# Sums over heads in two rounded passes, square sums on VectorE, and a final norm by square root and reciprocal, in a two-layer hybrid decoder trunk

## The chip, the cores and the metric

The kernel runs on one core of a Trainium2 chip. A core has TensorE (PE in the profile; its weight loads are listed apart as PEld), VectorE (DVE), ScalarE (ACT), GpSimd (POOL) and SyncE (SP), which here issues all DMAs. The metric is the device time of one execution in microseconds (us), as the median of several runs.

## The reference

Two layers, each with three token mixers on the same normalised input, then a last norm over the channels. Cut to what the change touches:

```python
def rms_norm(x, w):                      # at the start of a layer, and at the end
    y = xf * lax.rsqrt(jnp.mean(xf * xf, axis=-1, keepdims=True) + EPS)
    return (y * w).astype(x.dtype)

def head_norm(y, eps): ...               # retention: 4 heads of 256 channels
# RWKV, 16 heads of 64 channels:
    kk = hd(k * k_k)
    kk = kk / jnp.maximum(jnp.linalg.norm(kk, axis=-1, keepdims=True), 1e-12)
    bonus = (jnp.sum(rh * kh * r_k, axis=-1, keepdims=True) * vh)

def reference(x, ...):                   # x: 1 x 512 x 1024, float32
    for l in range(2):
        x = hybrid_layer(x, ...)         # one input projection, RG-LRU, RWKV-7, retention, output projection
    return rms_norm(x, final_norm_w)
```

## The kernel before

Activations lie with channels on the 128 partitions and the 512 tokens in the free dimension, so a row of 1024 channels is eight tiles of 128x512. A projection is eight 128x128 weight tiles against eight activation tiles. Weights and activations are split into a rounded high half and the remainder (`whi`, `wlo`; `hh`, `hl`; in the first four projections `xh`, `xl`), both in the reduced type fp32r, and each product is three matmuls: high by high, high by low, low by high. The splitting is done on the way: ScalarE copies the raw weights to `whi`, VectorE subtracts to get `wlo`. A projection is therefore 24 matmuls of 128x512.

Sums over channels run over partitions, so TensorE does them, by a matmul against a matrix of ones (`ones`) or of two 64x64 blocks of ones (`blk`). In the kernel before these take plain fp32 operands: `kss` (square norm of k per RWKV head, 16 in all), `bps` (the bonus sum, 16), `rss` (square sum of a retention head, 8) and `ss` (the square sum of a norm: 3 per norm, and two times 3 halves at the end).

Every operation is recorded through one helper, so all rows of the profile carry one line (L368 before, L378 after); the tile's name tells what it is. A planner (the class Scheduler) gives each operation a cost in the code, plays the program through by these costs, and writes the instructions of each engine out in the order that comes of it. The engines then run their own lists in order and wait by semaphores. The table `ORDER` names the order in which the pieces are recorded: `p` prepares a pair of RWKV head tiles, `s` scores, `c` its chain over chunks, `o` its output, `l` a group of RG-LRU, `r` a retention head, `b` a branch projection, and `g` two of the 24 merge gates computed ahead and stored in DRAM; nine `g` of twelve stand in the table.

At the start, `sum_sq` squares the eight tiles of x (ScalarE) and adds them to three partial sums, in layer 0 by GpSimd; three `ss` matmuls sum these; ScalarE turns the result into `rs` by Ln and Exp. Meanwhile the first four projections run on `xh`, `xl`, whose low halves VectorE makes, and are scaled by `rs` later. At the end, the last output tile is projected in two halves of 256 tokens. Each half is added to the residual (VectorE), squared (ScalarE), summed (`ss`), turned to `rs` by Ln and Exp, which are in different function tables, and then eight tiles of the half are scaled (six on VectorE, two on GpSimd) and stored.

Of the kernel before, what the change touches and what calls it, by code (L numbers as in the profile page):

```python
# [64 lines left out]

ORDER = "p0 l1 s0 g5 l0 g7 p1 g6 c0 l2 o0 g4 s1 p2 g2 g3 c1 o1 l3 s2 r0 r1 p3 g11 c2 r2 g10 o2 s3 r3 c3 g9 o3 b0 b2 b1".split()

# [84 lines left out]
class Scheduler:  # L156


    def __init__(self, nc):
        self.nc, self.pools, self.caps = nc, {}, {}  # L160
        self.ops, self._group, self._prio = [], None, 4
        self.fifo = {}

    def add_pool(self, name, pool, cap):
        self.pools[name] = pool
# [6 lines left out]
    @contextmanager  # L172
    def prio(self, p):
        old, self._prio = self._prio, p
        yield
        self._prio = old

    @contextmanager
    def group(self):
# [19 lines left out]
    def _commit(self, items):  # L199
        op = Op()  # L200
        op.i, op.eng, op.prio = len(self.ops), items[0][0], self._prio
        assert all(x[0] == op.eng for x in items)
        op.cost = sum(x[2] for x in items)
        op.calls = [(x[1], x[3], x[4]) for x in items]
        op.funcs = [x[7] for x in items if x[7]]
        op.mode = items[0][8]
        op.succ, op.ready, op.allocs, op.tiles = [], 0.0, [], []
        deps = set()
        for x in items:
            for ap in x[6]:  # L210
                self._access(op, ap, False, deps)
            for ap in x[5]:
                self._access(op, ap, True, deps)
        deps.discard(op)
        op.ndep = len(deps)
        for d in deps:
            d.succ.append(op)
        self.ops.append(op)
# [154 lines left out]
def hybrid_kernel(ctx: ExitStack, tc: tile.TileContext, xT, wt, par, cst, outT):  # L373
# [13 lines left out]
    def once(pool, name, shape, dt=F32):  # L387
        S.caps[pool][name] = 1
        return S.tile(pool, shape, dt, name, tag=name)
# [67 lines left out]
    def f32(ap):  # L457
        return ap.bitcast(F32)


    cs = once("c", "cs", [P, NRES])
    ident = cs[:, C_ID:C_ID + P]
    ones = cs[:, C_ONE:C_ONE + P]
    blk = cs[:, C_BLK:C_BLK + P]
    blkc = cs[:, C_BLKC:C_BLKC + P]
    cos = cs[:, C_COS:C_COS + T]
    sin = cs[:, C_SIN:C_SIN + T]
# [2 lines left out]
    ders = [once("c", f"der{l}", [P, NDC]) for l in range(DEPTH)]  # L470
    bcol = once("c", "bcol", [P, 4])
    warm = once("c", "warm", [P, 1])
    gsc = [once("dram", f"gs{l}", [24, P, T]) for l in range(DEPTH)]
    ysc = {(l, b): once("dram", f"ys{l}{b}", [KT, P, T]) for l in range(DEPTH) for b in range(3)}
    xsc = once("dram", "xsc", [KT, P, T])

    def pcol(l, n, i):
        return pars[l][:, POFF[n] + i:POFF[n] + i + 1]
# [6 lines left out]
    def setup():  # L485
# [21 lines left out]
                tt(lo[:, cc], raw[:, cc], f32(hi[:, cc]), ALU.subtract)  # L507
        first = hi, lo
        dma(cs[:, :C_COS], cst[:, :C_COS], P * C_COS * 4)
        dma(cs[:, C_COS:], cst[:, C_COS:NRES], P * (NRES - C_COS) * 4)  # L510
        dma(pars[1][:], par[1], P * NPC * 4)
        memset("DVE", reset[:, 0:T:CH], 0.0)
# [196 lines left out]
    def retention(l, h, n):  # L709
# [39 lines left out]
        with S.prio(3):  # L749
# [21 lines left out]
                sqs.append(sq)  # L771
            ps = tl("d", "rss")
            tt(sqs[0][:], sqs[0][:], sqs[1][:], ALU.add)
            mm(ps[:], ones, sqs[0][:], True, True, T)
            rs = sqs[0]
            act(rs[:], ps[:], ACTF.Ln, scale=1.0 / 256, bias=bcol[:, 3:4])
            act(rs[:], rs[:], ACTF.Exp, scale=-0.5)
# [34 lines left out]
    def rwkv_prep(l, la, rkv, g):  # L812
# [9 lines left out]
        for i, j in enumerate(js):  # L822
# [12 lines left out]
            thw.append(two[0])  # L835
            tha.append(two[1])
            s = tl("tp", "ksq")
            act(s[:], k[i][:], ACTF.Square, scale=pcol(l, "k_k", j))
            ps = tl("rp", "kss")
            mm(ps[:], blk, s[:], True, True, T)  # L840
            ts(thw[i][:], thw[i][:], 1.0, None, ALU.add)
            S.rec("DVE", nc.vector.tensor_tensor_scan, 1.25,
                  dict(out=thw[i][:], data0=reset[:], data1=thw[i][:], initial=0.0, op0=ALU.mult, op1=ALU.add))
# [17 lines left out]
    def rwkv_scores(l, prep, g):  # L861
# [75 lines left out]
            TB.append(tb)  # L937
        for i, j in enumerate(js):
            ps = tl("rp", "bps")
            mm(ps[:], blk, r[i][:], True, True, T)  # L940
            b = tl("tc", "bonus")
            tt(b[:], ps[:], v[i][:], ALU.mult)
            bonus.append(b)
# [213 lines left out]
    for l in range(DEPTH):  # L1157
        with S.prio(1):
            xw = gained(l, xs)
            ps = sum_sq(xs, ptt if l == 0 else tt)  # L1160
        qs = [tl("tm", "q") for _ in range(4)]
        early = [proj(l, w, xw, bank, wts=first if l == 0 and w == W_LA else None)
                 for w, bank in zip((W_LA, W_K, W_R, W_V), "aaad")]
# [76 lines left out]
    with S.prio(0):  # L1240
# [8 lines left out]
                tt(acc[k % 2][:], acc[k % 2][:], sq[:], ALU.add)  # L1249
        gain = [pcol(0, "final_norm_w", k) for k in range(KT)]  # L1250
        k, wts, rs = KT - 1, weights(l, W_OUT + KT - 1), tl("tm", "rs")
        for hf in range(2):
            cols = slice(256 * hf, 256 * hf + 256)
            ps = proj(l, None, ms, "ad"[hf], wts=wts, cols=cols)
            tt(xs[k][:, cols], xs[k][:, cols], ps[:, cols], ALU.add)
            act(sq[:, cols], xs[k][:, cols], ACTF.Square)
            act(warm[:], sq[:, 256 * hf:256 * hf + 1], ACTF.Ln, scale=0.0, bias=bcol[:, 0:1])
            ps = tl("rp", "ss")
            for n, a in enumerate(acc):
                mm(ps[:, cols], ones, a[:, cols], n == 0, n == 2, 256)  # L1260
            act(rs[:, cols], ps[:, cols], ACTF.Ln, scale=1.0 / D, bias=bcol[:, 0:1])
            act(rs[:, cols], rs[:, cols], ACTF.Exp, scale=-0.5)
            for i in range(KT):
                if i % 4 == 1:
                    if hf == 0:
                        act(xs[i], xs[i], ACTF.Identity, scale=gain[i])
                    ptt(xs[i][:, cols], xs[i][:, cols], rs[:, cols], ALU.mult)
                else:
                    stt(xs[i][:, cols], xs[i][:, cols], gain[i], rs[:, cols], ALU.mult, ALU.mult)
                dma(outT[i][:, cols], xs[i][:, cols], TILE_B // 2)  # L1270

    with tc.manual_schedule():
# [77 lines left out]
```

## Time and profile before

| | before |
|---|---|
| time, median of 3 runs (range) | 1973.65 us (1973.26 to 1974.21) |
| time of the profiled execution | 1973.38 us |
| its span in the profile | 1971.6 us |
| PE busy / DVE / ACT / POOL, share of the span | 99% / 64% / 46% / 29% |
| VectorE, busy us and instructions | 1262.5, 1887 |
| ScalarE, busy us and instructions | 914.1, 1384 |
| loads of function tables on ScalarE | 101, 1283 ns each |

A busy share is an average over the whole span; which engine sets the pace at a place is read from the idle time there and from what ended it. Matmuls are pipelined: the profile draws one longer than its turn, so the price of a matmul is read from the distance between starts. A plain fp32 matmul is issued in two parts, so it counts as two rows of the profile. The profiled execution lasts 1.8 us longer than its span.

### The profile page before, as it was taken

Reading aid. Unit: us, or ns where it says so; the run is one execution under the profiler, and the core shown is the slowest. Engines: PE = TensorE matmul, PEld = TensorE weight load, DVE = VectorE, ACT = ScalarE, POOL = GpSimd, SP = SyncE. Lnnn points to the kernel's source line nnn. Section 1 sums busy time; section 2 is a strip of 40 time slices with the busy share of each in tenths; the row PEclk is TensorE's granted clock in tenths of the full one; section 3 lists DMA queues with packets and bytes.
Section 4 is the critical chain, followed back from the end, with each engine's and each line's share of the span. In section 5 each row is a group of like instructions: output and inputs, shape, how many; then the busy total and the mean of one; then the engine's idle time right before and its main releaser. Section 6 shows DMA issues by size and latency. Waiting matters only on the chain.

```text
span 1971.6 us, 32177 instructions
## 1 busy us (share of the span) xinstructions
PE 1947.8 (99%) x12822; PEld 1544.9 (78%) x12822; DVE 1262.5 (64%) x1887; ACT 914.1 (46%) x1384; POOL 574.4 (29%) x797
## 2 busy tenths in 40 slices
PE   8999999999999999999999999999999999999997
PEld 5788778877787888788878887788787878777886
DVE  8894676667645855365569847756685468544554
ACT  6763753554325434242357638335534452434333
POOL 3138122612541154000012452253317121720000
PEclk9999999999999999999999999999999999999999
DMA  4233233322231325264522331333132313434642
GB/s 153 91 110 126 73 108 111 115 73 82 82 119 54 105 73 160 89 228 133 176 94 94 123 118 64 111 107 113 49 100 96 103 50 111 134 98 140 219 144 75
DMA packets 110981, 217.08 MB, mean 110 GB/s; under 512 B 43376, under 2 KB 46704, under 8 KB 110832
## 3 DMA queue, kind: packets, MB, share of 16 engines
q1 hardware_dynamic: 110832, 215.03, 33.7%
q8 instruction: 101, 1.65, 0.3%
q14 instruction: 48, 0.39, 0.1%
HBM read 184.58 MB, written 30.41 MB: 109 GB/s over the span
## 4 chain that ended last, share of the span: by engine, by line
PE 95%; DVE 3%; issue 0%; ACT 0%; DMA 0%; SPq 0%; DVEq 0%; ACTq 0%
PE acc L368 71%; PE p L368 5%; PE vp L368 5%; PE gate L368 2%; PE rsc L368 2%; PE sc L368 2%; PE rout L368 2%; PE w L368 2%; PE yt L368 1%; PE vt L368 1%; PE lora L368 1%; PE tr L368 1%; PE bps L368 1%; PE kss L368 1%; DVE wlo L368 0%
## 5 line engine op out<-in xcount | busy, mean ns | idle before, releaser
L368 PE MATMUL acc<-hh,whi 128*128 128x512 f32 x1488 | 604.8, 406 | 0.0
L368 ACT ACTIVATE whi<-raw 128x1024 fp32r<-128x1024 f32 (+1 forms) x283 | 298.8, 1056 | 638.0 <-PE acc L368 519.8
L368 PE MATMUL acc<-hh,wlo 128*128 128x512 f32 x1488 | 581.3, 391 | 1.3 <-DVE wlo L368 1.3
L368 PE MATMUL acc<-hl,whi 128*128 128x512 f32 x1488 | 580.4, 390 | 0.0
L368 DVE TENSOR_TENSOR wlo<-raw,whi 128x1024 fp32r<-128x1024 f32 (+1 forms) x283 | 358.3, 1266 | 186.7 <-ACT whi L368 183.4
L368 PEld LDWEIGHTS acc<-hh,whi 128*128 128x128 f32 x1488 | 279.3, 188 | 68.5 <-issue 7.2
L368 PEld LDWEIGHTS acc<-hh,wlo 128*128 128x128 f32 x1488 | 279.3, 188 | 62.1 <-DVE wlo L368 2.2
L368 PEld LDWEIGHTS acc<-hl,whi 128*128 128x128 f32 x1488 | 279.7, 188 | 57.2 <-issue 4.3
L368 POOL TENSOR_TENSOR etmp<-ex,ea 64x31 f32<-64x31 f32 (+15 forms) x248 | 170.2, 686 | 44.6 <-DMA ea<-ead 25.8
L368 POOL TENSOR_TENSOR dec<-sv,pc 64x128 f32<-64x128 f32 x96 | 50.3, 524 | 438.5 <-DVE sv L368 434.9
L368 POOL TENSOR_TENSOR ex<-ex,etmp 64x31 f32<-64x31 f32 (+15 forms) x248 | 168.8, 681 | 19.4
L368 ACT ACT_TABLE_LOAD x101 | 129.6, 1283 | 3.4 <-DVE pc L368 0.9
L368 PE MATMUL acc<-yh,whi 128*128 128x512 f32 x256 | 104.1, 407 | 0.0
L368 PE MATMUL acc<-yh,wlo 128*128 128x512 f32 x256 | 100.2, 391 | 0.0
L368 PE MATMUL acc<-ylo,whi 128*128 128x512 f32 x256 | 99.9, 390 | 0.0
L368 POOL TENSOR_TENSOR bk<-k,pi 64x512 f32<-64x512 f32 x32 | 50.9, 1589 | 162.7 <-DVE k L368 147.9
L368 PE MATMUL acc<-mq,whi 128*128 128x512 f32 (+1 forms) x272 | 79.9, 377 | 0.0
L368 PE MATMUL acc<-yq,whi 128*128 128x512 f32 x256 | 78.8, 389 | 0.0
L368 PE MATMUL vp<-whi,hh 128*128 128x256 f32 x256 | 78.2, 305 | 0.0
L368 DVE TENSOR_SCALAR sv<-p 64x128 f32<-64x128 f32 x64 | 18.8, 295 | 90.7 <-ACT sv L368 71.9
L368 PE MATMUL vp<-whi,hl 128*128 128x256 f32 x256 | 72.3, 282 | 0.0
L368 PE MATMUL vp<-wlo,hh 128*128 128x256 f32 x256 | 72.3, 282 | 0.0
(229 smaller groups left out, 3168.9 us busy)
## 6 DMA issues: line engine op xcount, KB each, us to landing
raw<-in_w SPq DMA_DIRECT2D x281, 512.0 KB, 3.3
yl<-ys SPq DMA_DIRECT2D x48, 256.0 KB, 4.8
gs<-thm SPq DMA_DIRECT2D x36, 256.0 KB, 2.3
thm<-gs SPq DMA_DIRECT2D x36, 256.0 KB, 4.0
ys<-thg SPq DMA_DIRECT2D x16, 256.0 KB, 2.5
ys<-bonus SPq DMA_DIRECT2D x16, 256.0 KB, 2.4
ys<-yr SPq DMA_DIRECT2D x16, 256.0 KB, 2.4
x<-in_x SPq DMA_DIRECT2D x8, 256.0 KB, 4.3
```

The source lines that it names most:

```text
L368: fn(*[r(v) for v in pos], **{k: r(v) for k, v in kw.items()})
```

## The change

Four things change. (1) A function `column_sums` does the sums `kss`, `bps` and `rss` with a high half `csh` (ScalarE) and a remainder `csl` (VectorE), both fp32r, in two matmuls against `picks`, an fp32r copy of the matrices of ones made once at the start. The `ss` sums stay as they are. (2) The square sums of layer 0 are added by VectorE. (3) The final norm takes Sqrt on ScalarE and a reciprocal on VectorE; the scalings of both halves are recorded behind both sums, and `behind` holds VectorE's scalings so that all but the first two of half 0 stand behind the addition of half 1. (4) `ORDER` places other gates elsewhere: nine `g` as before, with g1 in the place of g9. The remaining diff:

```diff
-ORDER = "p0 l1 s0 g5 l0 g7 p1 g6 c0 l2 o0 g4 s1 p2 g2 g3 c1 o1 l3 s2 r0 r1 p3 g11 c2 r2 g10 o2 s3 r3 c3 g9 o3 b0 b2 b1".split()
+ORDER = "p0 l1 s0 g5 l0 g11 g7 g6 p1 c0 l2 o0 g4 s1 g3 g1 p2 c1 o1 l3 s2 r0 r1 p3 c2 r2 g10 o2 s3 g2 r3 c3 o3 b0 b2 b1".split()
...
+        if self._behind is not None and self._behind.eng == op.eng:
+            deps.add(self._behind)
...
+    def column_sums(ps, w, s, pool, hi=None):
+        if hi is None:
+            hi = tl(pool, "csh", dt=F32R)
+            act(hi[:], s, ACTF.Copy)
+        lo = tl(pool, "csl", dt=F32R)
+        tt(lo[:], s, f32(hi[:]), ALU.subtract)
+        with S.group():
+            mm(ps, w, hi[:], True, False, T)
+            mm(ps, w, lo[:], False, True, T)
...
+        act(picks[:], cs[:, C_ONE:C_ONE + 2 * P], ACTF.Copy)
...
-            mm(ps[:], ones, sqs[0][:], True, True, T)
+            column_sums(ps[:], onesr, sqs[0][:], "tm")
...
+            act(hi[:], k[i][:], ACTF.Square, scale=pcol(l, "k_k", j))
-            mm(ps[:], blk, s[:], True, True, T)
+            column_sums(ps[:], blkr, s[:], "tp", hi)
...
-            mm(ps[:], blk, r[i][:], True, True, T)
+            column_sums(ps[:], blkr, r[i][:], "tp")
...
-            ps = sum_sq(xs, ptt if l == 0 else tt)
+            ps = sum_sq(xs, tt)
...
-            act(warm[:], sq[:, 256 * hf:256 * hf + 1], ACTF.Ln, scale=0.0, bias=bcol[:, 0:1])
+            if hf == 0:
+                act(warm[:], sq[:, 0:1], ACTF.Sqrt)
...
-            act(rs[:, cols], ps[:, cols], ACTF.Ln, scale=1.0 / D, bias=bcol[:, 0:1])
-            act(rs[:, cols], rs[:, cols], ACTF.Exp, scale=-0.5)
+            act(rs[:, cols], ps[:, cols], ACTF.Sqrt, scale=1.0 / D, bias=bcol[:, 0:1])
+            S.rec("DVE", nc.vector.reciprocal, 0.45, dict(out=rs[:, cols], in_=rs[:, cols]))
+        for hf, cols in enumerate(halves):
...
-                    stt(xs[i][:, cols], xs[i][:, cols], gain[i], rs[:, cols], ALU.mult, ALU.mult)
+                    with S.behind(added[1] if hf == 0 and i > 2 else added[0]):
+                        stt(xs[i][:, cols], xs[i][:, cols], gain[i], rs[:, cols], ALU.mult, ALU.mult)
```

In the order of the instructions it looks so at three places. First, TensorE at the first `kss` of layer 0, before, between the last matmul of one projection and the first of the next:

```order
L368 MATMUL acc_609<-hh_454,whi_573 128x512
L368 MATMUL acc_609<-hl_467,whi_573 128x512
L368 MATMUL acc_609<-hh_454,wlo_587 128x512
L368 MATMUL kss_651<-ksq_641,cs_214 128x512
L368 MATMUL acc_655<-hh_340,whi_616 128x512
L368 MATMUL acc_655<-hl_357,whi_616 128x512
```

and now:

```order
L378 MATMUL acc_611<-hh_417,wlo_586 128x512
L378 MATMUL acc_657<-hh_319,whi_618 128x512
L378 MATMUL acc_657<-hl_346,whi_618 128x512
L378 MATMUL acc_657<-hh_319,wlo_628 128x512
L378 MATMUL acc_657<-hh_348,whi_618 128x512
L378 MATMUL acc_657<-hl_360,whi_618 128x512
L378 MATMUL acc_657<-hh_348,wlo_628 128x512
L378 MATMUL kss_668<-csh_646,picks_244 128x512
L378 MATMUL kss_668<-csl_655,picks_244 128x512
```

The one fp32 matmul has become two fp32r matmuls, and they stand six projection matmuls later. Second, the start of the program on VectorE, from the third low half of x on (`sq` the square sums, `sp` and `der` small constants), before:

```order
L368 SCALAR_TENSOR_TENSOR xl_173<-x_121,par0_139,xh_165 128x512
L368 TENSOR_SCALAR der0_150<-par0_139 128x8
L368 TENSOR_SCALAR der0_150<-par0_139 128x24
L368 TENSOR_TENSOR sp0_152<-par0_139,sp0_152 128x8
L368 SCALAR_TENSOR_TENSOR xl_193<-x_133,par0_139,xh_176 128x512
L368 TENSOR_SCALAR sp0_152<-sp0_152 128x8
L368 SCALAR_TENSOR_TENSOR xl_200<-x_133,par0_139,xh_195 128x512
L368 TENSOR_TENSOR wlo_157<-raw_136,whi_147 128x512
L368 SCALAR_TENSOR_TENSOR xl_216<-x_145,par0_139,xh_203 128x512
```

and now, from the same low half up to the last one but one:

```order
L378 SCALAR_TENSOR_TENSOR xl_173<-x_121,par0_139,xh_164 128x512
L378 TENSOR_TENSOR sq_141<-sq_141,sq_170 128x512
L378 SCALAR_TENSOR_TENSOR xl_190<-x_133,par0_139,xh_176 128x512
L378 TENSOR_TENSOR sq_160<-sq_160,sq_181 128x512
L378 SCALAR_TENSOR_TENSOR xl_198<-x_133,par0_139,xh_192 128x512
L378 TENSOR_TENSOR wlo_157<-raw_136,whi_147 128x512
L378 SCALAR_TENSOR_TENSOR xl_214<-x_145,par0_139,xh_200 128x512
L378 TENSOR_TENSOR sq_141<-sq_141,sq_202 128x512
L378 SCALAR_TENSOR_TENSOR xl_223<-x_145,par0_139,xh_216 128x512
L378 TENSOR_TENSOR sq_141<-sq_141,sq_221 128x512
L378 TENSOR_TENSOR sq_160<-sq_160,sq_212 128x512
L378 TENSOR_TENSOR wlo_240<-raw_179,whi_225 128x1024
```

Five additions of squares have come between the low halves, and the small constants have gone behind them; the low half of the next weights (`wlo_240`) now stands ahead of the last two low halves of x. On TensorE the three `ss` matmuls, which stood behind all 24 matmuls of the first projection, now stand behind 18 of them, and the first six matmuls of the second projection come before the last six of the first. Third, the end of the program on VectorE (`xr` the residual tiles, of which each name holds two), before:

```order
L368 TENSOR_TENSOR xr_17245<-xr_17245,acc_17472 128x256
L368 SCALAR_TENSOR_TENSOR xr_17245<-xr_17245,par0_139,rs_17519 128x256
L368 SCALAR_TENSOR_TENSOR xr_17218<-xr_17218,par0_139,rs_17519 128x256
L368 SCALAR_TENSOR_TENSOR xr_17230<-xr_17230,par0_139,rs_17519 128x256 x2
L368 SCALAR_TENSOR_TENSOR xr_17233<-xr_17233,par0_139,rs_17519 128x256
L368 TENSOR_TENSOR xr_17245<-xr_17245,acc_17512 128x256
L368 SCALAR_TENSOR_TENSOR xr_17245<-xr_17245,par0_139,rs_17519 128x256
```

and now:

```order
L378 RECIPROCAL rs_17721<-rs_17721 128x256
L378 SCALAR_TENSOR_TENSOR xr_17420<-xr_17420,par0_139,rs_17721 128x256
L378 SCALAR_TENSOR_TENSOR xr_17432<-xr_17432,par0_139,rs_17721 128x256
L378 TENSOR_TENSOR xr_17447<-xr_17447,acc_17714 128x256
L378 SCALAR_TENSOR_TENSOR xr_17432<-xr_17432,par0_139,rs_17721 128x256
L378 SCALAR_TENSOR_TENSOR xr_17435<-xr_17435,par0_139,rs_17721 128x256
L378 SCALAR_TENSOR_TENSOR xr_17447<-xr_17447,par0_139,rs_17721 128x256
L378 RECIPROCAL rs_17721<-rs_17721 128x256
```

The addition of half 1 (the second TENSOR_TENSOR before, the only one now) stood behind five scalings of half 0 and stands behind two, and each half's `rs` is finished by a reciprocal. Behind the rows shown stand six more scalings before, and seven now. On ScalarE four table loads around these norms have become one.

## Rows read from the trace of the kernel before

**Rows 1.** The page, part 1: busy us, share, instructions.
```profile
PE 1947.8 (99%) x12822; PEld 1544.9 (78%) x12822; DVE 1262.5 (64%) x1887; ACT 914.1 (46%) x1384; POOL 574.4 (29%) x797
```
**Rows 2.** The chain that ended last, by engine.
```profile
PE 95%; DVE 3%; issue 0%; ACT 0%; DMA 0%; SPq 0%; DVEq 0%; ACTq 0%
```
**Rows 3.** Busy time by stretch: start:end, length, PE, PEld, DVE, ACT, POOL, granted clock, DMA.
```profile
10.00:20.00 10.00, 6.34 (x15) 3.64 (x14) 10.00 (x12) 7.89 (x14) 7.25 (x5) 0.66 0.54 194
80.00:100.00 20.00, 20.00 (x110) 16.14 (x109) 19.80 (x29) 14.89 (x21) 3.78 (x2) 1.00 0.32 103
60.00:1000.00 940.00, 938.63 (x6264) 746.24 (x6263) 601.14 (x878) 436.98 (x663) 276.13 (x389) 1.00 0.34 111
1020.00:1940.00 920.00, 918.77 (x6181) 730.74 (x6181) 585.25 (x857) 422.02 (x641) 273.48 (x388) 1.00 0.34 109
```
**Rows 4.** TensorE around the first kss: start, us, instruction.
```profile
63.64 0.40 PE L368 MATMUL acc<-hh,wlo 128*128 128x512 f32 x1
63.87 1.02 PE L368 MATMUL kss<-ksq,cs 128*128 128x512 f32 x2
...
64.97 0.40 PE L368 MATMUL acc<-hl,whi 128*128 128x512 f32 x1
```
**Rows 5.** The chain in order of time, one piece near the end of layer 0.
```profile
858.64 126.71 PE acc L368 x558
```
**Rows 6.** The three sums by tile: count of parts, ns, first and last start.
```profile
L368 PE MATMUL kss<-ksq,cs x32: 590/592/697, 63.9 to 1580.3; 128*128 128x512 f32 x32
L368 PE MATMUL bps<-r,cs x32: 592/592/593, 137.9 to 1682.7; 128*128 128x512 f32 x32
L368 PE MATMUL rss<-ysq,cs x16: 590/592/697, 456.6 to 1701.8; 128*128 128x512 f32 x16
```
**Rows 7.** Groups by line, the split of another tile: busy, mean ns, idle before.
```profile
L368 ACT ACTIVATE cvh<-cv 128x512 fp32r<-128x512 f32 x16 | 10.1, 629 | 29.8 <-DVE cv L368 29.8
L368 DVE TENSOR_TENSOR cvl<-cv,cvh 128x512 fp32r<-128x512 f32 x16 | 12.4, 778 | 6.1 <-ACT cvh L368 6.1
```
**Rows 8.** GpSimd, VectorE and TensorE at the start, in order of time.
```profile
12.02 5.59 POOL L368 TENSOR_TENSOR sq<-sq 128x512 f32<-128x512 f32 x3 [0.35 <-ACT sq L368]
...
7.04 0.69 DVE L368 TENSOR_TENSOR wlo<-raw,whi 128x512 fp32r<-128x512 f32 x1
...
12.28 1.25 DVE L368 TENSOR_SCALAR sp<-sp 128x8 f32<-128x8 f32 x1
13.44 0.74 DVE L368 SCALAR_TENSOR_TENSOR xl<-x,par,xh 128x512 fp32r<-128x512 f32 x1
...
14.70 4.77 DVE L368 SCALAR_TENSOR_TENSOR xl<-x,par,xh 128x512 fp32r<-128x512 f32 x4
...
23.82 0.40 PE L368 MATMUL acc<-xl,whi 128*128 128x512 f32 x1
```
**Rows 9.** ScalarE, VectorE and TensorE at the end, in order of time, by engine.
```profile
1954.77 0.46 ACT L368 ACTIVATE rs<-ss,bcol 128x256 f32<-128x256 f32 x1
...
1960.36 0.42 ACT L368 ACTIVATE sq<-xr 128x256 f32<-128x256 f32 x1 [3.40 <-DVE xr L368]
...
1956.99 3.00 DVE L368 SCALAR_TENSOR_TENSOR xr<-xr,par,rs 128x256 f32<-128x256 f32 x5 [4.18 <-ACT rs L368]
1959.92 0.41 DVE L368 TENSOR_TENSOR xr<-xr,acc 128x256 f32<-128x256 f32 x1
...
1964.50 3.50 DVE L368 SCALAR_TENSOR_TENSOR xr<-xr,par,rs 128x256 f32<-128x256 f32 x6 [3.78 <-ACT rs L368]
...
1957.09 0.28 PE L368 MATMUL acc<-mq,wlo 128*128 128x256 f32 x1
1960.83 0.70 PE L368 MATMUL ss<-sq,cs 128*128 128x256 f32 x2 [3.45 <-ACT sq L368]
```
**Rows 10.** The small constants by tile: count, ns (least, median, most), first and last start.
```profile
L368 DVE TENSOR_TENSOR sp<-sp x20: 154/167/169, 21.0 to 56.1; 128x8 f32<-128x8 f32 x20
...
L368 DVE RECIPROCAL sp<-sp x2: 196/199/202, 20.7 to 47.5; 128x8 f32<-128x8 f32 x2
```

More of the change, by code (lines that the diff above doesn't have):

```diff
@@ L162, in __init__ @@
         self.fifo = {}
+        self._behind = None
     def add_pool(self, name, pool, cap):
@@ L176, in prio, with behind @@
         self._prio = old
+    @contextmanager
+    def behind(self, op):
+        self._behind = op
+        yield
+        self._behind = None
     @contextmanager
@@ L463, in hybrid_kernel @@
     ones = cs[:, C_ONE:C_ONE + P]
-    blk = cs[:, C_BLK:C_BLK + P]
     blkc = cs[:, C_BLKC:C_BLKC + P]
@@ L472, in hybrid_kernel @@
     warm = once("c", "warm", [P, 1])
+    picks = once("c", "picks", [P, 2 * P], F32R)
+    onesr, blkr = picks[:, :P], picks[:, P:]
     gsc = [once("dram", f"gs{l}", [24, P, T]) for l in range(DEPTH)]
@@ L837, in rwkv_prep @@
             s = tl("tp", "ksq")
+            hi = tl("tp", "csh", dt=F32R)
             act(s[:], k[i][:], ACTF.Square, scale=pcol(l, "k_k", j))
+            act(hi[:], k[i][:], ACTF.Square, scale=pcol(l, "k_k", j))
             ps = tl("rp", "kss")
-            mm(ps[:], blk, s[:], True, True, T)
+            column_sums(ps[:], blkr, s[:], "tp", hi)
             ts(thw[i][:], thw[i][:], 1.0, None, ALU.add)
@@ L1251, in hybrid_kernel @@
         k, wts, rs = KT - 1, weights(l, W_OUT + KT - 1), tl("tm", "rs")
-        for hf in range(2):
-            cols = slice(256 * hf, 256 * hf + 256)
+        halves = [slice(0, 256), slice(256, 512)]
+        added = []
+        for hf, cols in enumerate(halves):
             ps = proj(l, None, ms, "ad"[hf], wts=wts, cols=cols)
             tt(xs[k][:, cols], xs[k][:, cols], ps[:, cols], ALU.add)
+            added.append(S.ops[-1])
             act(sq[:, cols], xs[k][:, cols], ACTF.Square)
-            act(warm[:], sq[:, 256 * hf:256 * hf + 1], ACTF.Ln, scale=0.0, bias=bcol[:, 0:1])
+            if hf == 0:
+                act(warm[:], sq[:, 0:1], ACTF.Sqrt)
             ps = tl("rp", "ss")
@@ L1260, in hybrid_kernel @@
                 mm(ps[:, cols], ones, a[:, cols], n == 0, n == 2, 256)
-            act(rs[:, cols], ps[:, cols], ACTF.Ln, scale=1.0 / D, bias=bcol[:, 0:1])
-            act(rs[:, cols], rs[:, cols], ACTF.Exp, scale=-0.5)
+            act(rs[:, cols], ps[:, cols], ACTF.Sqrt, scale=1.0 / D, bias=bcol[:, 0:1])
+            S.rec("DVE", nc.vector.reciprocal, 0.45, dict(out=rs[:, cols], in_=rs[:, cols]))
+        for hf, cols in enumerate(halves):
             for i in range(KT):
```

## The prediction

> **What bounds the kernel now.** I read the page first: TensorE is busy 99% of the span and no other engine passes 64% [rows 1]. A busy share alone proves little, since matmul rows overlap, so I went on to the chain of work that ended last: 95% of it is TensorE's [rows 2]. The third view is busy time by stretch. From 60 to 1000 us TensorE stands idle 1.4 us (940.00 less 938.63), from 1020 to 1940 us 1.2 us, at the full granted clock [rows 3]. So between the ramps at both ends TensorE's own work is the time: a microsecond of it removed is a microsecond gained, as long as its operands keep up, and a microsecond moved onto VectorE or ScalarE costs nothing where these have room. They have it on average (64% and 46%), but not everywhere: from 80 to 100 us VectorE is busy 19.80 of 20 us [rows 3]. The two ends are other regimes: at the start VectorE makes what TensorE waits for, and at the end a chain of single operations runs with TensorE idle.
>
> **The sums over heads.** In the timeline a matmul's price is the distance of starts. From the last projection matmul before the first `kss` to the second one after it, 1.33 us pass (63.64 to 64.97) [rows 4]. Without the sum these would be two ordinary distances; 558 projection matmuls in a row take 126.71 us, 0.227 each [rows 5]. So the fp32 sum costs 1.33 - 0.454 = 0.876 us, what there is of a change between fp32 and fp32r included. Now it is two fp32r matmuls of the same 128x512 shape, at 0.227 each as those in [rows 5], 0.454 together. Saved: 0.42 us. The profile has 32, 32 and 16 parts of `kss`, `bps` and `rss`, two parts to a sum, hence 40 sums [rows 6]; they last alike (592 ns median), so one price serves. **40 x 0.42 = 16.8 us.** The starts are rounded to 0.01 us; 0.40 and 0.43 per sum as bounds give 16.0 to 17.2.
>
> What this adds elsewhere: 40 high halves on ScalarE and 40 remainders on VectorE, for which the nearest rows are the same split of another tile, 629 and 778 ns [rows 7], about 25 and 31 us. The work that hides them is TensorE's projections, which need neither engine while they run; VectorE goes from 1262 to about 1297 us of 1953. I cost them at nothing. Were the cover gone, a sum would wait for its high half, its remainder and two handoffs, 1.4 us (0.63 + 0.78). At the first `kss` the planner has put six matmuls (6 x 0.227 = 1.36 us) between the sum's old place and its new one, which is about that chain. The gates set elsewhere by `ORDER` are nine stored pairs as before, so the same matmuls and DMAs, cost nothing; the bounds are the 2.6 us of idle time in the two long stretches, which could go, and new waits (below).
>
> **The start.** Before, GpSimd adds the squares until 17.6 us (12.02 + 5.59), and while it does VectorE is slow: a constant of 8 columns takes 1.25 us at 12.28 us, where an operation of that size otherwise takes 0.17 [rows 8, 10], and four low halves of x take 4.77 us where one alone takes 0.74 [rows 8]. With the additions on VectorE that ends: the four low halves alone give back 4.8 - 4 x 0.7 = 2.0 us and each stretched constant 1.1 us, and five additions cost, priced like a low half, 5 x 0.7 = 3.5 us. That is about even, so the last low half stays near 19.5 us (14.70 + 4.77). What changes is TensorE's order: the three fp32 `ss` matmuls fill the wait for the last two low halves. From 7.04 us [rows 8] VectorE has two half splits of weights, six low halves and five additions to do ahead of the sum, 13 x 0.66 = 8.6 us, so `ss` can start at 15.8 us, if the eighth square is there, as I assume. The granted clock of 10 to 20 us is 0.66 [rows 3], part of it at 1.2 GHz: TensorE had worked in bursts with waits between. The bursts stay about as they are, so I let the clock fall again until about 20 us; then `ss` takes three times 0.876 doubled, 5.2 us, to 21.0. Of the 48 matmuls of the first two projections 30 are then left. Before, TensorE was at the second matmul of the second projection at 23.82 us [rows 8], so it had 24 left at 23.6. Thirty left at 21.0 are 24 left at 22.4 (6 x 0.227). **Gain 1.2 us.** Bounds: nothing, if the squares come late; 3.8 us, if the clock is full while `ss` runs (2.6 us less).
>
> **The end.** The last matmul of half 1 ends at 1957.4 us, but its addition waits on VectorE behind five scalings of half 0 until 1959.92; then follow square, table load, Ln, table load and Exp, and the first scaling of half 1 starts at 1964.50, the sixth ends at 1968.0 [rows 9]. Now Sqrt starts where Ln did, 1954.77, and takes the same 0.46. The reciprocal of 256 columns has no row; the nearest is one of 8 columns, 199 ns against 167 for a plain operation of that size [rows 10]. If the 32 ns are fixed, 256 columns take the 0.41 of an addition of that width [rows 9] and 0.03, 0.45 us; if they grow with the columns (4 ns each), 0.41 + 256 x 0.004 = 1.45 us; by the widest pair of those rows (202 and 154 ns, 6 ns a column) 0.41 + 1.54 = 1.95 us. I take 1.45, the middle row of the same instruction. Then: reciprocal to 1956.7; two scalings of 0.60 (3.00 for five) to 1957.9; addition to 1958.3; square (0.42) to 1958.8; `ss` (0.70) to 1959.5; Sqrt (0.46) to 1960.0, with no table load left, while VectorE does three scalings; reciprocal to 1961.5; seven scalings at 0.58 (3.50 for six) to 1965.5, against 1968.0. **Gain 2.5 us.** With 0.45 for the reciprocal the addition can start at 1957.4 and the end is 1964.1, a gain of 3.9. Stores follow the last scaling as before.
>
> The Trainium skill (VectorE: DVE Perf Modes, First, the fixed hardware budget) says that the reciprocal is an iterated divide with a repeat count of 8; at the clock given there that would be an estimated 2.2 us for 256 columns. At 8 columns it would be about 58 ns above a plain operation; the row shows 32, so the trace bears it out by half.
>
> **Sum.** 16.8 + 1.2 + 2.5 = 20.5 us off the profiled execution's 1973.38 us: 1952.9 us. The median of the runs is 0.27 us above that execution, so I forecast **1953 us** for the median.
>
> **The rivals.** (a) *The reciprocal is slow by its width*, 1.95 us a half: the addition then ends at 1958.8, the second reciprocal runs from 1960.5 to 1962.4, the last scaling ends at 1966.5, and the end gains 1.5 instead of 2.5: 1954 us. For it: it is dearer at 8 columns already; against it: only by 32 ns in the middle. The Trainium skill's repeat count, quoted above, belongs to this rival; by its estimate of 2.2 us the end would gain 1.0. (b) *The ends give more*: full clock under `ss` (2.6 more) and a fixed reciprocal (1.4 more): 1949 us. For it: TensorE now waits less between the bursts; against it: 10 to 20 us were at 0.66 and the low halves still set the pace. (c) *Some sums wait for their remainder.* VectorE works in order, and the remainder may stand behind the split of a weight tile; at 0.25 us a sum 10 us are lost: 1963 us. For it: the full stretch at 80 to 100 us; against it: 1.4 and 1.2 us of idle time in all the rest of a program planned in the same manner. (d) *Slower:* the whole new chain of 1.4 us is exposed at each sum, on TensorE's path: 40 x 1.4 = 56 us, so about 2009 us; it decides from 20.5 / 40 = 0.5 us a sum on. Against it is the room of a third of VectorE's time and the later place of the sum. (e) *The two passes are no cheaper than the one*, because a change of operand type costs what they save: only the ends remain, 1969.6 us. Against it: the changes of type alone would have to make 0.42 of the 0.876 us of [rows 4].
>
> **How the numbers follow.** Forecast 0.50, (a) 0.20, (b) 0.12, (c) 0.12, (d) 0.04, (e) 0.02. The time is that of the likeliest. The low end takes (b) with the 2.6 us of idle time gone: 1953 - 4.0 - 2.6 = 1946.4. The high end is (c), 1963, rounded down to 1962, since most of (c) lies lower. The likeliest case alone spans 1950 to 1956. A change of 0.2%, 3.9 us, is about what measurement tells from none. Slower by more than that is (d), 0.03 of it; the same is the rest of (d), a far end of (c) and part of (e), 0.03; faster is all else, 0.94.
>
> **What would show it.** Right: `kss`, `bps` and `rss` as two matmuls each 0.23 us apart, 0.42 us less around each; TensorE idle from 60 to 1940 us still under 5 us; the first scaling of half 1 some 3 us earlier than 1964.50; VectorE's 8-column operations at 0.17 us before 20 us. Wrong: waits of TensorE for `csl`, or for `wlo` where a `csl` stands ahead of it; a reciprocal that takes over 2 us; `ss` at 0.43 us a pass and the first projection ending after 24 us. The prediction falls if idle time on TensorE grows by over 10 us, wherever it lies.

## The result and the profile after

The changed kernel takes 1960.38 us (median of 4 runs, 1959.80 to 1961.27) where the kernel before takes 1973.56 in the same session: ratio 0.9935, 95% interval 0.9922 to 0.9948, 13.2 us less. The forecast was 1953, with 1946.5 to 1962 as its range: the sign and the range hold, but a third of the 20.5 us is missing.

The page, part 1, of the changed kernel:

```profile
PE 1932.9 (99%) x12822; PEld 1541.6 (79%) x12822; DVE 1296.6 (66%) x1934; ACT 907.9 (46%) x1403; POOL 552.1 (28%) x792
```

And its busy time by stretch, columns as in [rows 3]:

```profile
10.00:20.00 10.00, 9.04 (x30) 5.36 (x31) 8.65 (x25) 9.96 (x16) 0.00 (x0) 1.00 0.80 282
80.00:100.00 20.00, 19.07 (x104) 15.30 (x103) 19.75 (x28) 15.50 (x21) 7.06 (x8) 1.00 0.28 92
60.00:1000.00 940.00, 935.28 (x6277) 747.58 (x6276) 623.63 (x902) 435.67 (x674) 272.85 (x391) 1.00 0.34 111
1020.00:1926.00 906.00, 901.89 (x6135) 720.95 (x6134) 596.10 (x871) 418.02 (x648) 265.73 (x388) 1.00 0.34 109
```

TensorE has 14.9 us less work than in [rows 1]. But it now stands idle 4.7 us from 60 to 1000 and 4.1 us in the stretch of layer 1, where [rows 3] had 1.4 and 1.2. From 10 to 20 us the granted clock is 1.00, where it was 0.66. Whom TensorE waits for, in the list of waits (us in total, times, longest), in layers and ends together:

```profile
PE p L378 <- DVE zs L378: 3.4, 5, 0.9
PE sc L378 <- POOL bk L378: 1.9, 2, 0.9
PE ss L378 <- ACT sq L378: 1.8, 1, 1.8
PE acc L378 <- DVE xl L378: 1.7, 5, 0.5
PE p L378 <- DVE sv L378: 1.6, 2, 0.8
...
PE acc L378 <- DVE wlo L378: 1.1, 2, 0.6
PE gate L378 <- DVE cvl L378: 0.9, 2, 0.5
```

In the kernel before, the same list has only two rows that lie in the layers:

```profile
PE p L368 <- DVE zs L368: 2.2, 2, 1.1
PE acc L368 <- DVE wlo L368: 1.3, 2, 0.7
```

No row says that a sum waits for `csl` or `csh`, and the wait for `wlo` has not grown. The new waits are those of the chain (`p`, 5.0 us in all where it was 2.2), of the scores (`sc`), where GpSimd's `bk` is late, and of the LRU gates. The sums themselves do what was forecast; TensorE in order of time at the first `kss`, to be read beside [rows 4]:

```profile
59.63 0.40 PE L378 MATMUL acc<-hh,wlo 128*128 128x512 f32 x1
59.87 0.39 PE L378 MATMUL kss<-csh,picks 128*128 128x512 f32 x1
60.10 0.39 PE L378 MATMUL kss<-csl,picks 128*128 128x512 f32 x1
60.33 0.40 PE L378 MATMUL acc<-hh,whi 128*128 128x512 f32 x1
60.56 0.40 PE L378 MATMUL acc<-hl,whi 128*128 128x512 f32 x1
```

59.63 to 60.56 is 0.93 us where 1.33 us passed before: 0.40 less. The start, VectorE and TensorE in order of time, beside [rows 8]:

```profile
16.73 0.24 DVE L378 TENSOR_SCALAR der<-par 128x8 f32<-128x8 f32 x2
18.17 0.75 DVE L378 SCALAR_TENSOR_TENSOR xl<-x,par,xh 128x512 fp32r<-128x512 f32 x1 [0.92 <-ACT xh L378]
...
14.47 2.84 PE L378 MATMUL ss<-sq,cs 128*128 128x512 f32 x6
...
34.85 0.39 PE L378 MATMUL acc<-hh,whi 128*128 128x512 f32 x1
```

And the end, VectorE and ScalarE, beside [rows 9]:

```profile
1943.82 1.75 DVE L378 RECIPROCAL rs<-rs 128x256 f32<-128x256 f32 x1 [2.36 <-ACT rs L378]
1945.61 1.35 DVE L378 SCALAR_TENSOR_TENSOR xr<-xr,par,rs 128x256 f32<-128x256 f32 x2
1946.88 0.41 DVE L378 TENSOR_TENSOR xr<-xr,acc 128x256 f32<-128x256 f32 x1
1947.21 1.40 DVE L378 SCALAR_TENSOR_TENSOR xr<-xr,par,rs 128x256 f32<-128x256 f32 x3
1949.03 1.75 DVE L378 RECIPROCAL rs<-rs 128x256 f32<-128x256 f32 x1 [0.42 <-ACT rs L378]
1950.70 3.70 DVE L378 SCALAR_TENSOR_TENSOR xr<-xr,par,rs 128x256 f32<-128x256 f32 x7
...
1948.53 0.47 ACT L378 ACTIVATE rs<-ss,bcol 128x256 f32<-128x256 f32 x1 [0.79 <-PE ss L378]
```

To compare kernels, the span is cut into three: the *start* up to TensorE's first matmul with `hh`, the *middle* from there to the first `ss` matmul of the final norm, and the *end*. *Idle* is TensorE's idle time ahead of the middle's matmuls, added up. It is a lower bound of the waits: a projection matmul is drawn 0.39 us long while the next may start 0.23 us after it, so each wait hides up to 0.16 us. Medians and ratios are over all runs, the three parts are of the one profiled execution, which can lie off its kernel's median: 2.4 us below it for sums_own3, 1.8 to 2.3 us above it for sums_only, after_prices and best. All kernels below stand here once:

| kernel | us | ratio to before (95%) | start | middle | idle | end |
|---|---|---|---|---|---|---|
| before | 1973.56 | | 39.96 | 1912.23 | 3.9 | 19.42 |
| changed | 1960.38 | 0.9935 (0.9922 to 0.9948) | 34.85 | 1905.99 | 9.9 | 17.17 |
| sums_only | 2014.40 | 1.0204 (1.0187 to 1.0221) | 40.63 | 1953.94 | 42.6 | 19.82 |
| order_only | 1977.31 | 1.0015 (1.0006 to 1.0025) | 39.37 | 1916.22 | 7.1 | 19.42 |
| start_only | 1968.78 | 0.9975 (0.9964 to 0.9985) | 35.57 | 1911.86 | 3.7 | 19.43 |
| end_only | 1971.36 | 0.9986 (0.9977 to 0.9996) | 40.54 | 1911.91 | 3.9 | 17.23 |
| sums_own3 | 1972.36 | 0.9993 (0.9984 to 1.0003) | 39.16 | 1909.57 | 13.5 | 19.44 |
| same_order_no_csl | 1959.66 | 0.9930 (0.9915 to 0.9945) | 35.27 | 1904.94 | 9.1 | 17.18 |
| same_order_two_csl | 1967.70 | 0.9971 (0.9960 to 0.9983) | 35.35 | 1913.58 | 13.3 | 17.17 |
| same_order_fp32_sums | 1975.68 | 1.0011 (1.0002 to 1.0020) | 35.83 | 1921.02 | 9.2 | 17.17 |
| same_order_no_recip | 1957.86 | 0.9921 (0.9906 to 0.9936) | 35.76 | 1906.68 | 10.3 | 14.50 |
| after_prices | 1978.39 | 1.0028 (1.0017 to 1.0039) | 35.48 | 1926.48 | 19.9 | 16.85 |
| own3_prices_old_order | 1970.74 | 0.9986 (0.9977 to 0.9995) | 35.80 | 1915.52 | 12.9 | 16.86 |
| best | 1958.43 | 0.9925 (0.9913 to 0.9938) | 35.80 | 1908.41 | 8.6 | 14.39 |

So the change won 5.1 us at the start (forecast 1.2), 2.25 at the end (forecast 2.5), and 6.2 in the middle (forecast 16.8). The middle is what has to be explained.

### The profile page after: what moved, and what is told of

It reads as the page before. It is cut to its first block, busy times and chain, and to the rows that moved or that the text cites. A ratio compares the mean times of both kernels' runs of the same rounds, so it can differ in the third digit from the quotient of the medians.

```text
span 1958.0 us, 32282 instructions
## 1 busy us (share of the span) xinstructions
PE 1932.9 (99%) x12822; PEld 1541.6 (79%) x12822; DVE 1296.6 (66%) x1934; ACT 907.9 (46%) x1403; POOL 552.1 (28%) x792
## 5 line engine op out<-in xcount | busy, mean ns | idle before, releaser
L378 DVE TENSOR_TENSOR wlo<-raw,whi 128x1024 fp32r<-128x1024 f32 (+1 forms) x283 | 362.3, 1280 | 239.7 <-ACT whi L378 236.8
L378 POOL TENSOR_TENSOR etmp<-ex,ea 64x31 f32<-64x31 f32 (+15 forms) x248 | 161.0, 649 | 42.2 <-DMA ea<-ead 23.4
L378 ACT ACT_TABLE_LOAD x82 | 105.2, 1283 | 2.2 <-PEq L1371 0.7
L378 POOL TENSOR_TENSOR hl<-hf,hh 128x512 fp32r<-128x512 f32 x8 | 16.2, 2035 | 211.0 <-ACT hh L378 211.0
```

What stands on the lines that cost most here:

```text
L378: fn(*[r(v) for v in pos], **{k: r(v) for k, v in kw.items()})
```

## The experiments

**Each part alone.** Theory 1: VectorE's 40 remainders make it late where it is full, and TensorE waits there. Theory 2: the new `ORDER` brings the waits. Theory 3: the planner writes another order after any edit, and waits come with it. The first kernel takes all of `column_sums` and `picks` into the kernel before, the others one line or one block each:

```diff
 # sums_only
+            column_sums(ps[:], blkr, s[:], "tp", hi)
-            mm(ps[:], blk, s[:], True, True, T)
 # order_only: the new ORDER; start_only:
-            ps = sum_sq(xs, ptt if l == 0 else tt)
+            ps = sum_sq(xs, tt)
 # end_only: the block of the final norm and behind()
```

> The kernel before with column_sums and picks alone; ORDER, square sums and final norm as before. Theory 1 (the 40 remainders make VectorE late at its full stretches, so TensorE waits at other operations): about 16 us less in TensorE's own work and 8 to 10 us of new waits at sc, gate and p, so 1966 to 1968 us. Theory 2 (the new ORDER brings the waits): no new waits, 1957 to 1958 us. Theory 3 (every edit makes the planner write another order, and waits come and go with it): anything between, with waits at other places than in the changed kernel.

> The kernel before with the new ORDER alone. Theory 1: within 2 us of 1973.6 us. Theory 2: 8 to 10 us slower, 1982 to 1984 us, with waits at sc near 91 us and at gate near 123 us. Theory 3: off by some 2 to 5 us either way.

> The kernel before with the square sums of layer 0 on VectorE alone. If the start's gain is its own (full granted clock from 10 to 20 us): 5 us less, 1968.5 us, with the first product of hh near 35 us. By the prediction's step (clock falls again): 1.2 us less, 1972.4 us. Theories 1 and 2: no new waits in the middle. Theory 3: the middle moves by 2 us or more, though no instruction there was changed.

> The kernel before with the final norm by Sqrt and reciprocal and with the additions ahead of the scalings, alone. All theories of the middle: 2.2 to 2.5 us less, 1971.2 us, the reciprocal of 256 columns 1.75 us as in the changed kernel. Theory 3: the middle moves as well.

The two ends are independent: start_only gives 4.8 us (1973.64 less 1968.78, the median of before in that session), end_only 2.3, and neither touches the middle (0.4 us at most). That speaks against theory 3 in its widest form: an edit at an end leaves the middle alone. order_only costs 3.7 us, inside the range of theory 3 and of no other. And sums_only, the part from which most of the gain was to come, is 41 us *slower*, which no theory had. Alone the four parts add up to +37; together they give -13. The sums and the new `ORDER` are no independent edits. In sums_only the loss lies in a few places. Busy time by stretch there:

```profile
270.00:290.00 20.00, 19.42 (x181) 14.86 (x180) 12.02 (x18) 9.11 (x16) 8.96 (x9) 1.00 0.33 119
290.00:310.00 20.00, 7.43 (x48) 6.01 (x50) 17.13 (x29) 2.95 (x6) 3.93 (x4) 0.64 0.19 59
310.00:320.00 10.00, 10.00 (x51) 7.91 (x50) 5.67 (x12) 0.61 (x2) 0.94 (x2) 0.70 0.01 2
```

And two of TensorE's waits in that stretch, in order of time:

```profile
301.81 1.94 PE L368 MATMUL tr<-cs,bk 128*128 128x128 f32 x8 [3.99 <-DVE bk L368]
307.71 0.79 PE L368 MATMUL sc<-se,bk 64*128 64x128 f32 x2 [3.96 <-POOL bk L368]
```

For 20 us TensorE has nothing but the scores of one group and their transposes: no projection stands between, and each step waits for VectorE or GpSimd. On top the granted clock falls to 0.64 and stays at 0.70 after the stall, so part of the work behind it runs at 1.2 GHz: projection matmuls start 0.43 us apart from 312.0 to 315.8 us, and 0.23 apart from 316.1 on. Both come again in layer 1.

**Where the projections went.** A pool hands its buffers out in the order in which tiles are recorded: the planner lets an instruction take a buffer only if its tile is the first in the pool's queue (`if n >= len(free[k]) or n >= len(f) or f[n] is not t: return None`). `csh` and `csl` stand in the queues of `tp` and `tm`, which the inputs of other stages also use. Theory 4: that queue, and not the work, makes the hole.

```diff
-    caps = {"h": 16, "tp": 16, "tc": 6, "tm": 16, ...
+    caps = {"h": 16, "tp": 16, "tc": 6, "tm": 14, ..., "ch": 3}
-            hi = tl(pool, "csh", dt=F32R)
+            hi = tl("ch", "csh", dt=F32R)
-        lo = tl(pool, "csl", dt=F32R)
+        lo = tl("ch", "csl", dt=F32R)
```

> The kernel before with column_sums and picks and its own ORDER, as in sums_only, but the halves csh and csl in three buffers of their own instead of the shared pools tp and tm (tm gives up two of its 16). Theory 4 (the loss of sums_only comes from the queue for buffers: each pool hands its buffers out in the order in which tiles are recorded, and csh and csl stand in that queue ahead of what the projections need): the stretch near 283 to 310 us with nothing but score matmuls on TensorE is gone, 1965 to 1978 us. Theory 1 (VectorE's and ScalarE's added work does it): the added work is the same, so it stays within 10 us of 2014 us. Theory 2 (the old ORDER does it): 2014 us as well.

1972.36 against 2014.40: 42 us come back with the same instructions, the same old `ORDER` and only other buffers. Theory 4 stands for the loss of sums_only, and theories 1 and 2 fall there. (That the tiles' place in the queue does it is read from the planner's code; the run shows that the buffers alone decide.) The middle without idle time is now 1909.57 - 13.47 = 1896.1 us, as in the changed kernel (1905.99 - 9.95 = 1896.0), and 12.2 less than before (1908.3). But 13.5 us of idle time remain, so the sums gain little net here: 1.0 us by the median against the kernel before in the same session, 2.7 in the middle of the trace.

**One engine's work changed, every order kept.** To separate what an engine has to do from the order in which the planner puts it, three kernels keep the changed kernel's order of instructions on every engine and alter one thing as the instructions are written out:

```diff
+                if kw["out"].t.name == "csl": continue               # no_csl
+                if kw["rhs"].t.name == "csl": kw = dict(kw, rhs=op.calls[0][1]["rhs"])
...
+                for _ in range(1 + (kw["out"].t.name == "csl")):     # two_csl
...
+                if kw["rhs"].t.name == "csl": continue               # fp32_sums
+                if kw["rhs"].t.name == "csh":
+                    kw = dict(kw, lhsT=kw["lhsT"].bitcast(F32), rhs=kw["rhs"].bitcast(F32), stop=True)
```

> The changed kernel with every engine's instructions in the order in which they stand there, but the 40 subtractions csl left out, and the second matmul of each sum reading csh again (the sums then lack their remainder): TensorE's work is the same, VectorE has some 30 us less. Theory 1 (the new waits come from VectorE's added work): 7 to 9 us less, 1952 to 1954 us, no wait at sc near 91 us, TensorE idle under 3 us from 60 to 1000. Theory 3 (the waits belong to the arrangement that the planner wrote, whatever VectorE does): within 2.5 us of 1960.4 us, the waits at sc, gate and p still there.

> The changed kernel with every instruction in the order in which it stands there, but each of the 40 subtractions csl done twice: some 30 us more on VectorE. Theory 1: the waits at the full stretches grow by what is added there, at least 8 us more, 1968 us or above. Theory 3: VectorE has room, 1960 to 1963 us.

> The changed kernel with every instruction in the order in which it stands there, high halves and subtractions included, but each of the 40 sums as one fp32 matmul again, of the high half alone (the sums then lack their remainder): only TensorE's work differs, by 40 times 0.42 us, 16.8 us. If the new waits belong to the arrangement, whatever TensorE does: 16 to 17 us more than the changed kernel, 1976 to 1977.5 us, with the waits at sc, gate and p as they are. If they are the time saved at the sums, handed back where VectorE, ScalarE and GpSimd set the pace (TensorE now comes too early there): only 7 to 11 us more, 1967 to 1971 us, and the waits at sc near 91 us, at gate and at p shrink or are gone.

Without the 40 subtractions the time is 1959.66 us, 0.7 less, which is hardly to be told from nothing. TensorE's list of waits in that kernel:

```profile
PE p L382 <- DVE zs L382: 2.8, 4, 0.9
...
PE sc L382 <- POOL bk L382: 1.9, 2, 0.9
...
PE p L382 <- DVE sv L382: 1.6, 2, 0.8
...
PE gate L382 <- DVE cvl L382: 0.9, 2, 0.4
```

They are the waits of the changed kernel, less one `p` on `zs` (2.8 us where it was 3.4). Theory 1 falls. But the room is thin: with the subtractions done twice the time is 7.3 us more, since the next 30 us on VectorE do show. Theory 3's "1960 to 1963" misses that by far, and theory 1's "1968 us or above" only by 0.3: the second 30 us behave as theory 1 had it for the first. In the sums' own rows TensorE now waits for a remainder (`PE rss L379 <- DVE csl L379: 0.5, 2, 0.3` stands in its list).

With fp32 sums again in the same order the middle is 1921.02 - 1905.99 = 15.0 us longer, 0.376 us a sum, and the total 15.3 us longer (16 to 17 if the waits belong to the arrangement, 7 to 11 if they are time handed back). Its waits:

```profile
PE p L382 <- DVE zs L382: 3.3, 5, 0.9
PE sc L382 <- POOL bk L382: 1.9, 2, 1.0
...
PE p L382 <- DVE sv L382: 0.9, 2, 0.4
PE gate L382 <- DVE cvl L382: 0.9, 2, 0.5
```

TensorE comes 15 us later to the end and waits at the same places as long, except at one `p` of each layer (0.44 instead of 0.79 us). So the time saved at the sums is not handed back at the waits; they belong to the arrangement. This kernel also prices it: TensorE has the same matmuls as in the kernel before, and the middle is 1921.02 - 1912.23 = 8.8 us longer. With the -15.0 of the sums that makes the -6.2 of the middle; it is no check, since the 8.8 is the remainder. It holds all else that the change does there: the place of every instruction, the subtractions (0.7 us above) and the 40 high halves on ScalarE, which no run took out alone. Of the 8.8 us, 5.3 are idle time (9.2 against 3.9). For the other 3.5 the traces name no wait; hidden waits could make them, or changes between kinds of operand, since TensorE goes back from fp32 to fp32r 293 times there and 269 times before (counted in the traces). Which of the two it is stays open, as no run prices a change alone. Two executions of the same middle differ by up to 0.7 us (changed, same_order_no_recip).

**The reciprocal.** Again every order kept; Sqrt and reciprocal of the final norm become one activation.

```diff
+                if fn == self.nc.vector.reciprocal and kw["out"].size == 256: continue
+                if kw.get("func") == ACTF.Sqrt and kw["out"].t.name in ("rs", "warm"):
+                    kw = dict(kw, func=ACTF.Abs_reciprocal_sqrt)
```

> The changed kernel with every instruction in the order in which it stands there, but rs of the final norm made by one activation (Abs_reciprocal_sqrt) where Sqrt and a reciprocal on VectorE stood. If the reciprocal stands on the path at both halves: half 0 gives 0.8 us (the addition of half 1 then waits for TensorE), half 1 the 1.75 us of the reciprocal, 2.5 us together, 1957.9 us. If only the second counts: 1.75 us, 1958.6 us. If the activation brings table loads that the warming does not cover: nothing or up to 2.5 us more, 1960 to 1963 us.

1957.86 us, 2.5 less, as worked out for a reciprocal that stands on the path at both halves. VectorE's end in order of time:

```profile
1945.41 1.36 DVE L382 SCALAR_TENSOR_TENSOR xr<-xr,par,rs 128x256 f32<-128x256 f32 x2 [2.36 <-ACT rs L382]
1947.65 0.42 DVE L382 TENSOR_TENSOR xr<-xr,acc 128x256 f32<-128x256 f32 x1 [0.88 <-PE acc L382]
1947.99 1.67 DVE L382 SCALAR_TENSOR_TENSOR xr<-xr,par,rs 128x256 f32<-128x256 f32 x4
1949.82 3.49 DVE L382 SCALAR_TENSOR_TENSOR xr<-xr,par,rs 128x256 f32<-128x256 f32 x6 [0.17 <-ACT rs L382]
```

The addition of half 1 now waits for TensorE alone, and the second `rs` costs VectorE 0.17 us of waiting.

**Prices.** If the waits are planned in, are they planned on wrong prices? The planner believes that `bk` on GpSimd lasts 1.39 us; the trace has 1.62. The next kernels give it the durations of the changed kernel's trace; the second also has the old `ORDER` and the three buffers of sums_own3, the third these buffers, another `ORDER` and the one activation of same_order_no_recip.

```diff
+        if aps_w and eng in ("DVE", "ACT", "POOL"):
+            cost = PRICE.get(f"{eng} {aps_w[0].t.name} {getattr(aps_w[0], 'size', 0)}", cost - 0.05)
```

> The changed kernel, its ORDER and its computation as they are; only the planner's prices for VectorE, ScalarE and GpSimd are set to the mean durations that its own trace shows, less 0.05 us for the overlap of one instruction with the next (bk on GpSimd 1.57 instead of 1.39, r 1.14 instead of 0.73, bk on VectorE 0.82 instead of 0.68, and so on for 70 groups). Theory 3 in its narrower form (the new waits are operations that last longer than the planner believes, where TensorE's cover was planned to the tenth of a microsecond): the waits at sc near 91 us, gate near 123 us and p are planned away, 954 to 957 us above 1000, that is 1954 to 1957 us; a wait at a sum may come in their place. If prices have nothing to do with it: 1960 us or above, with waits of the same size at other places.

> The changed kernel with the ORDER of before, the measured prices of after_prices, and csh and csl in three buffers of their own (tm 14 instead of 16). Theory 4 with theory 3 (what the old ORDER lost in sums_only was the queue for buffers, and the rest prices): 1957 to 1964 us, 50 us below sums_only. Theory 2 (the split sums need the new ORDER as such): 1975 us or above.

> The changed kernel with everything that the runs so far point to: csh and csl in three buffers of their own, measured prices, rs of the final norm by one activation, and an ORDER chosen for these (p0 g4 l1 s0 g7 l0 g11 g6 p1 c0 g5 l2 o0 s1 g3 p2 c1 g10 g1 o1 and so on, again nine gates). If theories 3 and 4 are right: TensorE idle under 3 us from 60 to 1900 us as in the kernel before, the sums at 0.45 us each, 1947 to 1951 us. If waits come back whatever the prices: 1955 us or above.

All three miss what theories 3 and 4 had for them. after_prices is 18 us *slower* than the changed kernel: the wait at `sc` on `bk` is planned away, and others stand in its place, the longest at a sum. TensorE there in order of time:

```profile
645.18 0.51 PE L454 MATMUL rss<-csh,picks 128*128 128x512 f32 x1 [1.05 <-ACT csh L454]
648.36 0.79 PE L454 MATMUL rss<-csl,picks 128*128 128x512 f32 x1 [2.68 <-DVE csl L454]
```

And the stretch around it:

```profile
640.00:660.00 20.00, 15.62 (x69) 11.39 (x66) 11.79 (x15) 12.80 (x23) 7.24 (x7) 0.83 0.11 39
```

The granted clock of these 20 us is 0.83. In own3_prices_old_order the old `ORDER` with split sums takes 1970.74 us, 44 below sums_only (38 of them in the middle), which bears theory 4 out, but 7 us above what was expected. best keeps the buffers and the end and has fewer waits than the changed kernel (8.6 us idle), yet the middle of its trace is 2.4 us longer. The trace is of the slowest of its five executions, 2.3 us above their median, and in it TensorE stands idle before one `w` for no reason that the profile shows, with a granted clock of 0.72 from 200 to 206 us:

```profile
200.69 2.50 PE L454 MATMUL w<-xd,xw 128*64 128x32 f32 x64 [2.19 <-issue]
```

The clock is at its lower level for 3.4 us of these 6, of which half, 1.7 us, is lost (an estimate). The rest may be that its fp32 blocks stand next to each other less often: TensorE goes back from fp32 to fp32r 301 times, in the changed kernel 275 times. It has other waits, too (`PE acc L454 <- DVE wlo L454: 2.1, 2, 1.1`). Whether its median has a longer middle at all, the one trace can't tell. At 1958.43 us it can't be told from same_order_no_recip; these two are the quickest of the study, some 2 us ahead of the changed kernel and 15 ahead of the one before. Theory 3 in its narrow form, wrong prices, falls as a cure: two kernels with the measured prices are slower than the changed one, and the third is no quicker than same_order_no_recip, which kept the old prices.

## Why the prediction was right in sign and a third short

**Bound: TensorE's work is the time.** Right. With every order kept, 40 times a shorter sum came out as 15.0 us of 16.8.

**The sums, 16.8 us.** The mechanism is right, the size 12% too large and outside the stated 16.0 to 17.2: 0.376 us a sum by same_order_fp32_sums, 0.40 at the first `kss`, where 0.42 was taken. One place was read and taken for all 40. Rival (e), no cheaper passes, is out (its time, by its own terms, is 1969.8 and not 1969.6 us); so is (d), the whole chain exposed.

**"I cost them at nothing" (added work of VectorE and ScalarE).** For the remainders right in this arrangement: 0.7 us. The reason given, cover by projections, holds there, and rival (c), sums that wait for their remainder, does not show. It is nearer than I thought: in after_prices (2.7 us at an `rss`) and with doubled subtractions it does. For the high halves no run tells. ScalarE did not get fuller by them: the new plan loads 82 function tables where the old one loaded 101, at 1283 ns each, and its busy time fell from 914.1 to 907.9 us.

**`ORDER` at nothing: the step that failed.** I read off nine pairs as before and concluded that the same matmuls and DMAs take the same time. The work is the same, but its place decides what covers what. Alone the new `ORDER` costs 3.7 us. With the sums split and the halves in shared pools it is worth about 47 us: the old one with all other parts would be near 2014.4 - 4.9 - 2.3 = 2007, an estimate by addition that no run shows. And the arrangement that results costs 8.8 us in the middle against the one before; the 5.3 of it that are idle time lie at `p`, `sc` and gates, not at the sums. I had bounded new waits only at the sums and by the 2.6 us of idle time that *could go*, as if idle time elsewhere could only fall. The text's own signs caught it: TensorE was to stay idle under 5 us from 60 to 1940, and it stands idle for 4.7 + 4.1 us in the two stretches above, though not for 10 more than before. How the cost of the arrangement splits between the new `ORDER` (its middle alone is 4.0 longer) and the rest of the new plan stays open: any edit in the middle makes a new plan. What makes the single waits is read from the trace only. At `sc` near 92 us GpSimd's `bk` follows VectorE's `k` (the profile names `pc`, the copy just behind it), and VectorE is full:

```profile
79.46 1.17 DVE L378 SCALAR_TENSOR_TENSOR se<-ksq,pp 64x504 f32<-64x504 f32 x1
80.64 1.68 DVE L378 SCALAR_TENSOR_TENSOR so<-ksq,pp 64x504 f32<-64x504 f32 x1
...
87.76 0.69 DVE L378 TENSOR_TENSOR k<-k,lth 128x512 f32<-128x512 f32 x1
...
88.60 3.42 POOL L378 TENSOR_TENSOR bk<-k,pi 64x512 f32<-64x512 f32 x2 [4.71 <-DVE pc L378]
...
92.07 0.37 PE L378 MATMUL sc<-so,bk 64*128 64x128 f32 x1 [0.93 <-POOL bk L378]
```

**The start, 1.2 us taken, 5.1 measured** (4.4 in start_only's trace): mis-sized, and above its bound of 3.8. I let the granted clock fall as before; it stayed at 1.00, and `ss` took 2.84 us in place of 5.2. This is the first half of rival (b), to which 0.12 was given, and no luck: `ss` took 2.84 us in every trace with this start, also in same_order_fp32_sums, where the granted clock of 10 to 20 us is 0.89. The stretched constants are gone (0.24 us for two), the last `xl` starts at 18.17 and not near 19.5, and `ss` at 14.47 and not 15.8 (the sum as written gives 15.6). Part of that is luck. VectorE's first work waits for the parameters, and in this execution they came 0.6 us earlier; first the kernel before, then the changed one:

```profile
6.81 0.17 DVE L368 TENSOR_SCALAR der<-par 128x33 f32<-128x33 f32 x1 [5.37 <-DMA par<-in_p]
...
6.18 0.17 DVE L378 TENSOR_SCALAR der<-par 128x33 f32<-128x33 f32 x1 [4.74 <-DMA par<-in_p]
```

Counted from these rows the start gains 4.5 us. In the other traces of the changed kernel's order it ends at 35.3 to 35.8 us, in this one at 34.85.

**The end, 2.5 us taken, 2.25 measured.** The chain ran as written, with two errors that nearly cancel: the reciprocal of 256 columns took 1.75 us, between the 1.45 taken and the 1.95 of rival (a), and the last seven scalings took 3.70 us where 4.1 were taken. By [rows 10] and this row it grows by (1.75 - 0.20) / 248 = 6.2 ns a column. The estimate from the Trainium skill (VectorE: DVE Perf Modes, First, the fixed hardware budget), 2.2 us for a divide repeated 8 times, is too high by a quarter, but nearer than the 0.45 us of a fixed share; the 1.45 taken was nearer still.

Sum: 15.0 + 5.1 + 2.25 - 8.8 = 13.6 us, the difference of the two spans, as it must be, since the 8.8 is the remainder. That the time lies in the stated range is luck in part: the middle fell 10.6 us short of its 16.8, and with the ends as forecast that would be 1953 + 10.6, about 1964 us, outside it. The ends gave 3.7 us more than forecast and covered a third of the gap.

## What to carry to other kernels

Where one engine is busy 99% of the time, less work on it was the gain that held here, and a new order of everything else the part that no one had priced: price the two apart, by keeping every engine's order and changing one thing. A small new tile in a pool that hands out buffers in recorded order can cost more (42 us here) than the edit that needs it brings (15 us); give it buffers of its own, or move other work until the queue fits. A better price list did not make this planner's plan better by itself: measure the plan. And a total in the right place proves no term of the sum: here an error of 10.6 us and one of 3.7 us ran against each other.

## What the runs showed of the hardware

- In sums_only a stall of TensorE was paid for twice. The granted clock was 0.64 from 290 to 310 us and 0.70 in the ten behind them, though TensorE was busy for all of those ten. The middle without idle time is 1911.35 us there and 1896.10 in sums_own3, 15 us for the same matmuls. Some 13 of them are the clock, by an estimate: in the middle of that trace TensorE was busy for 26 us while the lower level was granted.
- Some of VectorE's operations stretch beside some of GpSimd's, in the middle as at the start. Of the changed kernel's 16 `r<-r,par,k`, 128x512, the eight with GpSimd idle took 0.74 to 0.75 us, and six that ran beside GpSimd's `bk` 1.77 to 1.79, as the one at 89.10 us; the kernel before took 0.74 there, at 90.09 us, with GpSimd idle. It is not so for all: `thg<-thg` took 0.69 us beside GpSimd's `ex` and `etmp`, and `sga<-sga,acc`, which reads a matmul's result, 0.68 beside `bk` (kernel before, 86.60 us). The planner's prices are one number for each operation and know nothing of this, which may be why better means did not help it; no run tried that alone.
- Abs_reciprocal_sqrt on 128x256 took 0.48 us on ScalarE at the end, where Sqrt (0.47) and a reciprocal on VectorE (1.75) stood.
